# Inverse norms of queries and keys on 16 columns a projection, and one reciprocal of four columns a head

## The chip, the cores and the metric

The kernel runs on one core of a Trainium2 chip. The metric is the device time of one execution in microseconds (us). TensorE is called PE below, VectorE DVE, ScalarE ACT, GpSimd POOL; SP is the engine that issues most DMAs.

## What is computed

One sequence of 512 rows and 1024 features goes through two transformer blocks in fp32. The first mixes by a pooling branch and by 12 heads of dilated attention, the second by 4 differential heads, 6 forgetting heads and 6 chunk heads. Cut to what the change touches:

```python
# first block: softmax over the keys, per head
e = jnp.exp(s - m); den = jnp.sum(e, axis=-1, keepdims=True)
o = jnp.einsum('brnhqk,brnkhd->brnqhd', e / den, vb)
# second block: every head's query and key is normed over its 64 features
q1 = rms_norm_2(split_heads(q1, H_DIFF), g[0])   # and q2, k1, k2, qf, kf, qc, kc
a = probs(q1b, k1) - lam * probs(q2b, k2)        # differential heads
pr = jax.nn.softmax(s, axis=-1)                  # forgetting and chunk heads
```

## The kernel before

**Stages.** The program runs mixer 1 (0 to 200 us of the span), its output projection (to 280), a feed-forward part (to 600 and 640), mixer 2 (640 to 905), its output projection (to 960) and a last feed-forward part with the gate. Products of fp32 are built from three matmuls each (high by high, high by low, low by high parts of the operands; lines 189 to 191 and 366 to 368), so weights are split into `wh` and `wl` as they come in (L166 on ACT, L170 on DVE or POOL).

**Mixers.** A play list, `ORDER1` or `ORDER2`, says in which order steps are written. In mixer 2 the part that matters below is `S00 S01 F P2 T3 P4 T2 VA W00 T4 S10 W01`: S is the scores of a head, P a projection of 256 columns of queries and keys (`project`), T its transposes into head form (`to_heads`, L310), V the values, W the weighing (`weigh`: transposes of the probabilities L277, then L285 and L286). The build then fixes one order of instructions for each engine; it may move an instruction ahead of one that was written earlier where their tiles allow it.

**Scores.** `probs` handles one block of 128 queries (qb = 0 to 3, with 128, 256, 384 or 512 keys): two matmuls (L255, L256), a masked negative row maximum on DVE (L259) into column 0 of a small tile, the exponential on ACT with its row sum into column 1, and a reciprocal of that one column on DVE (L263). `scale_rows` (L267) multiplies the block by it on POOL. Differential heads (S00 to S11) make two blocks a qb; the second is multiplied by lambda and subtracted on DVE (L707, L708).

**Norm of queries and keys.** In `project` of mixer 2, two of the four row tiles share a PSUM bank, so `out_of` is called twice a projection with 512 columns. Each call copies (L659) and squares (L660) on ACT, reduces the squares to 8 columns on DVE (L662), makes the inverse root of these 8 columns (L665 to L673 on DVE, Ln and Exp on ACT) and multiplies the copy `z` by it on POOL (L675). The transposes of T read `z`.

**Small tiles.** `small(w)` (L118) hands out tiles of w columns from a ring for each w: 16 buffers of 4 columns, 16 of 8 columns. A tile of one ring does not wait for one of another.

Of the kernel before, what the change touches and what calls it, by code (L numbers as in the profile page):

```python
# [11 lines left out]
AF = mybir.ActivationFunctionType  # L12
ALU = mybir.AluOpType
AX = mybir.AxisListType

P = 128
# [46 lines left out]
class Builder:  # L63
# [52 lines left out]
        self.special.append(i.ins.name)  # L116

    def small(self, w=4, dt=F32):  # L118
        return self.mp.tile([P, w], dt, tag=f"m{w}", name=self.nm("m"), bufs=16 if w < 16 else 3 if w < 64 else 1)

    def psum(self, wide=False):
        if wide:
# [123 lines left out]
        self.rsqrt(r, ps[:, 0:8], 1.0 / D, self.small(8))  # L246
        return r

    def probs(self, op, tab, qb, wide=False):
        nc = self.nc  # L250
        q1, k1, q2, k2 = op
        n = (qb + 1) * P
        c = slice(qb * P, qb * P + P)
        ps = self.psum() if wide else self.psS()
        nc.tensor.matmul(ps[:, :n], lhsT=q1[:, c], rhs=k1[:, :n], start=True, stop=False)  # L255
        nc.tensor.matmul(ps[:, :n], lhsT=q2[:, c], rhs=k2[:, :n], start=False, stop=True)  # L256
        p = self.slot("p")
# [6 lines left out]
        return p, m  # L264

    def scale_rows(self, p, m, n):
        self.nc.gpsimd.tensor_scalar(p[:, :n], p[:, :n], m[:, 2:3], 1.0, ALU.mult, ALU.mult)  # L267

    def weigh(self, ps_list, v, o, odd, wide=False):
        nc = self.nc  # L270
# [19 lines left out]
        nc.vector.tensor_tensor(o[a, :], pv[a, :], t[a, :], ALU.add)  # L290

    def scores(self, op, tab, wide=False):
        out = []
        for qb in range(4):
            p, m = self.probs(op, tab, qb, wide)
            self.scale_rows(p, m, (qb + 1) * P)
            out.append(p)
        return out

    def play(self, order, **steps):  # L300
# [314 lines left out]
    def mix2(self, h, rc):  # L615
        nc = self.nc
# [5 lines left out]
        r2 = self.const("r2", [P, 4])  # L622
        r1 = self.const("r1", [P, 4])
# [8 lines left out]
        lam = self.const("lam", [P, 4])  # L632
# [14 lines left out]
        ops = {}  # L647
# [5 lines left out]

        def project(i):
            out = zs[i] = []

            def out_of(t1, ps):
                z, sq = self.slot("z"), self.slot("z")
                nc.scalar.activation(z, ps, AF.Copy)  # L659
                nc.scalar.activation(sq, ps, AF.Square)  # L660
                st = self.small(8)
                nc.vector.tensor_reduce(st, sq.rearrange("p (h d) -> p h d", d=64), AX.X, ALU.add)  # L662
                four = lambda v: v[:, t1 - 1:t1 + 1].unsqueeze(2).to_broadcast([P, 2, 4])
                two = lambda v: v.rearrange("p (t h) -> p t h", h=4)
                nc.vector.tensor_tensor(two(st), two(st), four(r2), ALU.mult)  # L665
# [6 lines left out]
                nc.vector.tensor_tensor(two(y), two(y), four(r1), ALU.mult)  # L672
                nc.vector.tensor_tensor(st, y, w, ALU.mult)  # L673
                zv = z.rearrange("p (h d) -> p h d", d=64)
                nc.gpsimd.tensor_tensor(zv, zv, st.unsqueeze(2).to_broadcast([P, 8, 64]), ALU.mult)  # L675
                out.append(z)
# [14 lines left out]
        def table(name, src):  # L691
            t = self.slot("m")
            self.load_late(t, src)
            tabs[name] = t
            return t

        def score(i, e, wide=False):
            n, e = int(i), int(e)
            if n < 2:
                tab = table("a", io["tab_alibi"][2 * n + e])  # L700
                out = []
                for qb in range(4):
# [4 lines left out]
                    nc.vector.tensor_scalar(m2[:, 3:4], m2[:, 2:3], lam[:, 2:3], None, ALU.mult)  # L707
                    nc.vector.scalar_tensor_tensor(p1[:, :w], p2[:, :w], m2[:, 3:4], p1[:, :w],  # L708
                                                   ALU.mult, ALU.add)
# [48 lines left out]
        def early(m):  # L758
# [264 lines left out]
```

## Time and profile before

| what | us |
|---|---|
| runs | 1356.41, 1363.6, 1360.2 |
| median | 1360.2 |
| profiled execution, own time | 1363.75 |
| its span | 1362.0 |
| PE busy | 1319.5 |
| DVE busy | 862.6 |
| ACT busy | 674.2 |
| POOL busy | 205.5 |

The profile is one execution. Busy time is the union of an engine's instructions; a busy PE can still run at the lower of its two clock levels. The clock that was granted stands as PEclk, 1.00 being 2.4 GHz. A wait is written with the instruction that waited, the engine and line that released it, and its length.

### The profile page before, as it was taken

What the parts mean: (1) busy time and instruction counts of PE and PEld (TensorE: products, weight loads), DVE (VectorE), ACT (ScalarE), POOL (GpSimd) and SP (SyncE); (2) the same over time, 40 slices, a digit from 0 to 9 for tenths busy, and PEclk for the clock granted to TensorE, in tenths of its full rate; (3) what the DMA queues carried; (4) which work ended last, traced back from release to release, by engine and by line L of the source; (5) the groups of instructions that cost most, each with busy time, mean ns of one, the idle gap of its engine ahead of it and who ended that gap; (6) DMA issues with size and microseconds to landing.
All of it is one profiled execution on the core that took longest, in us unless ns stands there. A gap on an engine that the chain in (4) does not pass through costs nothing.

```text
span 1362.0 us, 20144 instructions
## 1 busy us (share of the span) xinstructions
PE 1319.5 (97%) x7450; PEld 1146.2 (84%) x7450; DVE 862.6 (63%) x1739; ACT 674.2 (50%) x1311; POOL 205.5 (15%) x240
## 2 busy tenths in 40 slices
PE   9899999999999999997999999999999999999998
PEld 9899878888888888886989999778888888888887
DVE  6777876864444432239678978666877777733345
ACT  6566756543333333236476778654644444522242
POOL 1233222300000000016222434331000000000010
PEclk9999999999999999998999999899999999999999
DMA  5422333233232233326333544332423332323222
GB/s 196 121 70 60 105 117 97 74 101 100 94 93 93 93 95 101 98 78 224 94 107 99 140 118 130 90 116 86 139 94 96 101 98 93 101 93 93 95 91 78
DMA packets 48802, 141.70 MB, mean 104 GB/s; under 512 B 6240, under 2 KB 7136, under 8 KB 48704
## 3 DMA queue, kind: packets, MB, share of 16 engines
q1 hardware_dynamic: 48704, 140.42, 33.1%
q8 instruction: 58, 0.95, 0.3%
q14 instruction: 40, 0.33, 0.1%
HBM read 122.38 MB, written 6.29 MB: 94 GB/s over the span
## 4 chain that ended last, share of the span: by engine, by line
PE 83%; DVE 10%; DMA 2%; issue 2%; ACT 2%; POOL 0%; SPq 0%; DVEq 0%; ACTq 0%; POOLq 0%
PE p L190 21%; PE p L189 21%; PE p L191 20%; PE p L368 5%; PE p L367 5%; PE p L366 5%; PE p L277 2%; DVE wl L170 1%; DVE sp L259 1%; DVE sv L573 1%; DVE sh L183 1%; PE p L286 1%; PE p L285 1%; PE p L255 1%; PE p L256 1%
## 5 line engine op out<-in xcount | busy, mean ns | idle before, releaser
L166 ACT ACTIVATE wh<-wr 128x512 fp32r<-128x512 f32 x417 | 260.0, 630 | 401.2 <-PE p L190 348.4
L170 DVE TENSOR_TENSOR wl<-wr,wh 128x512 fp32r<-128x512 f32 x398 | 287.7, 728 | 224.0 <-ACT wh L166 217.8
L190 PE MATMUL p<-sh,wh 128*128 128x512 f32 (+1 forms) x858 | 324.2, 379 | 7.7 <-DVE sh L183 7.6
L191 PE MATMUL p<-sh,wl 128*128 128x512 f32 (+1 forms) x858 | 323.5, 378 | 0.0
L189 PE MATMUL p<-sh,wh 128*128 128x512 f32 (+1 forms) x858 | 318.9, 377 | 0.1
L366 PE MATMUL p<-wh,sh 128*128 128x256 f32 (+1 forms) x736 | 211.2, 289 | 4.3 <-ACT sz L460 2.2
L368 PE MATMUL p<-wh,sh 128*128 128x256 f32 (+1 forms) x736 | 210.2, 288 | 5.2 <-DVE sh L183 5.2
L367 PE MATMUL p<-wl,sh 128*128 128x256 f32 (+1 forms) x736 | 210.6, 288 | 0.2
L190 PEld LDWEIGHTS p<-sh,wh 128*128 128x128 f32 x858 | 163.6, 191 | 39.6 <-DVE sh L183 9.0
L191 PEld LDWEIGHTS p<-sh,wl 128*128 128x128 f32 x858 | 163.7, 191 | 31.4 <-issue 0.7
L189 PEld LDWEIGHTS p<-sh,wh 128*128 128x128 f32 x858 | 161.8, 191 | 32.1 <-PE p L256 0.6
L368 PEld LDWEIGHTS p<-wh,sh 128*128 128x128 f32 x736 | 141.4, 193 | 7.3 <-DVE sh L183 6.4
L366 PEld LDWEIGHTS p<-wh,sh 128*128 128x128 f32 x736 | 141.9, 193 | 6.3 <-ACT sz L460 2.5
L367 PEld LDWEIGHTS p<-wl,sh 128*128 128x128 f32 x736 | 141.8, 193 | 1.4 <-DVE wl L170 0.6
L267 POOL TENSOR_SCALAR sp<-sp,m 128x128 f32<-128x128 f32 (+1 forms) x112 | 70.3, 631 | 161.8 <-DVE m L263 122.9
L170 POOL TENSOR_TENSOR wl<-wr,wh 128x512 fp32r<-128x512 f32 (+1 forms) x19 | 25.3, 1329 | 450.6 <-ACT wh L166 441.7
L114 ACT ACTIVATE sp<-sp,m 128x128 f32<-128x128 f32 (+3 forms) x128 | 71.5, 559 | 40.8 <-DVE m L259 37.6
L191 PE MATMUL p<-so,wl 128*128 128x512 f32 (+1 forms) x246 | 88.4, 360 | 0.3 <-DVE wl L170 0.3
L190 PE MATMUL p<-so,wh 128*128 128x512 f32 (+1 forms) x246 | 88.4, 360 | 0.0
L189 PE MATMUL p<-so,wh 128*128 128x512 f32 (+1 forms) x246 | 87.7, 361 | 0.5 <-DVE m L259 0.5
L259 DVE CUSTOM_DVE_ANT_0 sp<-p,sm 128x128 f32<-128x128 f32 (+3 forms) x128 | 60.2, 483 | 19.5 <-PE p L256 9.6
L190 PE MATMUL p<-sk,wh 128*128 128x512 f32 (+1 forms) x184 | 67.1, 365 | 0.0
(207 smaller groups left out, 2100.8 us busy)
## 6 DMA issues: line engine op xcount, KB each, us to landing
wr<-in_w_gu SPq DMA_DIRECT2D x88, 512.0 KB
wr<-in_w_down SPq DMA_DIRECT2D x44, 512.0 KB
wr<-in_w_qk SPq DMA_DIRECT2D x31, 512.0 KB
sk<-sk SPq DMA_DIRECT2D x88, 128.0 KB
wr<-in_w_out SPq DMA_DIRECT2D x12, 512.0 KB
sv<-in_x SPq DMA_DIRECT2D x16, 256.0 KB
wr<-in_w_ple_gate SPq DMA_DIRECT2D x8, 512.0 KB
wr<-in_w_v SPq DMA_DIRECT2D x6, 512.0 KB
```

The source lines that it names most:

```text
L114: i = self.nc.scalar.activation(out, in_, func, **k)
L166: nc.scalar.activation(hi[:, :w], c, AF.Copy)
L170: eng.tensor_tensor(lo[:, :w], c, hi[:, :w].bitcast(F32), ALU.subtract)
L189: mm(out, lhsT=ahi, rhs=bhi, start=start, stop=False)
L190: mm(out, lhsT=ahi, rhs=blo, start=False, stop=False)
L191: mm(out, lhsT=alo, rhs=bhi, start=False, stop=stop)
L259: nc.vector.tensor_tensor_reduce(p[:, :n], ps[:, :n], tab[:, (3 - qb) * P:S], 1.0, 3e38, ALU.add, ALU.min, accum_out=m[:, 0:1])
L267: self.nc.gpsimd.tensor_scalar(p[:, :n], p[:, :n], m[:, 2:3], 1.0, ALU.mult, ALU.mult)
L277: ins = nc.tensor.transpose(pt[:, w:w + P], ps_list[qb][:, kb * P:kb * P + P], self.ident)
L366: mm(d, lhsT=h[k][0][:, a], rhs=hi[:, c], start=k == 0 and (o == 0 or not first), stop=False)
L367: mm(d, lhsT=h[k][0][:, a], rhs=lo[:, c], start=False, stop=False)
L368: mm(d, lhsT=h[k][1][:, a], rhs=hi[:, c], start=False, stop=k == 7 and (o > 0 or not first))
```

## The change

`probs` gets a small tile and a column from its caller. `scores` takes one tile of 16 columns a head, lets the four blocks write maxima to columns 0 to 3 and sums to columns 4 to 7, makes one reciprocal of four columns into columns 8 to 11, and then issues the four multiplications on POOL. Differential heads take one such tile for each qb and make one reciprocal of two columns. `project` of mixer 2 takes one tile of 16 columns, each of the two calls of `out_of` reduces into half of it, and at the second call the inverse root is made once on 16 columns, after which both halves of `z` are multiplied. The tiles of 16 columns, those of heads and those of projections, are one ring of 8 buffers.

```diff
-        ... bufs=16 if w < 16 else 3 if w < 64 else 1)
+        ... bufs=16 if w < 16 else 8 if w < 24 else 3 if w < 64 else 1)
...
-    def probs(self, op, tab, qb, wide=False):
+    def probs(self, op, tab, qb, m, j, wide=False):
...
-        m = self.small(4)
-            accum_out=m[:, 0:1])
-        self.act(p[:, :n], p[:, :n], AF.Exp, bias=m[:, 0:1], scale=-1.0, accum_out=m[:, 1:2])
-        nc.vector.reciprocal(m[:, 2:3], m[:, 1:2])
+            accum_out=m[:, j:j + 1])
+        self.act(p[:, :n], p[:, :n], AF.Exp, bias=m[:, j:j + 1], scale=-1.0, accum_out=m[:, 4 + j:5 + j])
...
     def scores(self, op, tab, wide=False):
+        m = self.small(16)
+        out = [self.probs(op, tab, qb, m, qb, wide) for qb in range(4)]
+        self.nc.vector.reciprocal(m[:, 8:12], m[:, 4:8])
         for qb in range(4):
-            p, m = self.probs(op, tab, qb, wide)
-            self.scale_rows(p, m, (qb + 1) * P)
+            self.scale_rows(out[qb], m, qb, (qb + 1) * P)
...
         def project(i):
+            st = self.small(16)
...
-                st = self.small(8)
-                nc.vector.tensor_reduce(st, sq.rearrange("p (h d) -> p h d", d=64), AX.X, ALU.add)
+                nc.vector.tensor_reduce(st[:, 4 * t1 - 4:4 * t1 + 4], sq.rearrange("p (h d) -> p h d", d=64),
+                                        AX.X, ALU.add)
+                out.append(z)
+                if t1 < 3:
+                    return
...
-                y, w = self.small(8), self.small(8)
+                y, w = self.small(16), self.small(16)
...
-                nc.gpsimd.tensor_tensor(zv, zv, st.unsqueeze(2).to_broadcast([P, 8, 64]), ALU.mult)
+                for j in range(2):
+                    zv = out[j].rearrange("p (h d) -> p h d", d=64)
+                    nc.gpsimd.tensor_tensor(zv, zv, st[:, 8 * j:8 * j + 8].unsqueeze(2).to_broadcast([P, 8, 64]),
+                                            ALU.mult)
...
-                    p1, m1 = self.probs(ops[2 * n][e], tab, qb, wide)
-                    p2, m2 = self.probs(ops[2 * n + 1][e], tab, qb, wide)
-                    self.scale_rows(p1, m1, w)
+                    m = self.small(16)
+                    p1 = self.probs(ops[2 * n][e], tab, qb, m, 0, wide)
+                    p2 = self.probs(ops[2 * n + 1][e], tab, qb, m, 1, wide)
+                    nc.vector.reciprocal(m[:, 8:10], m[:, 4:6])
+                    self.scale_rows(p1, m, 0, w)
```

The instructions fall from 128 reciprocals to 40 and from 120 small DVE instructions of the norms to 60; 40 Ln and Exp instructions on ACT become 20. PE, POOL and SP have the same instructions as before. Their order is the same outside the two mixers.

**PE, end of P4, T2 and VA.** In the rows `p` is a PSUM tile, `sz` a z tile, `sp` a block of probabilities, `m` a small tile, `sk` queries or keys; the numbers are of each build alone. Before, from the last matmul of P4 on:

```order
L368 MATMUL p_7298<-wh_7241,sh_5739 128x256
L310 MATMUL p_7364<-ident,sz_7167 128x128 x2
L310 MATMUL p_7364<-ident,sz_7101 128x128 x2
L310 MATMUL p_7365<-ident,sz_7167 128x128 x2
L310 MATMUL p_7365<-ident,sz_7101 128x128 x2
L277 MATMUL p_7524<-ident,sp_6866 128x128
L277 MATMUL p_7524<-ident,sp_6885 128x128
L277 MATMUL p_7535<-ident,sp_6866 128x128
L277 MATMUL p_7535<-ident,sp_6885 128x128 x2
L255 MATMUL p_6949<-sk_6787,sk_6786 128x384
L256 MATMUL p_6949<-sk_6788,sk_6786 128x384
L255 MATMUL p_6960<-sk_6815,sk_6814 128x512
```

After, up to the first matmul of VA (L275 is the transpose of probabilities, L308 that of `z`, L364 the first of the three matmuls of a projection or of values):

```order
L275 MATMUL p_7530<-ident,sp_6794 128x128
L275 MATMUL p_7530<-ident,sp_6811 128x128
L275 MATMUL p_7541<-ident,sp_6811 128x128
L275 MATMUL p_7530<-ident,sp_6828 128x128
L275 MATMUL p_7541<-ident,sp_6828 128x128
L275 MATMUL p_7530<-ident,sp_6845 128x128
L275 MATMUL p_7541<-ident,sp_6845 128x128 x2
L308 MATMUL p_7221<-ident,sz_7035 128x128 x2
L308 MATMUL p_7221<-ident,sz_6981 128x128 x2
L308 MATMUL p_7222<-ident,sz_7035 128x128 x2
L308 MATMUL p_7222<-ident,sz_6981 128x128 x2
L364 MATMUL p_7253<-wh_7256,sh_5652 128x256
```

T2's eight transposes of `z` stood right behind P4 and ahead of the last three scores of S01; now they stand behind S01's last scores and behind the transposes of S01's four probability blocks (sp_6794 to sp_6845). VA's matmuls, which stood between and behind S01's last scores, follow T2 in both.

**DVE, the second square sum of P2.** Before (ISA is the masked maximum of a score block, from its PSUM tile and the table sm into sp and a column of m):

```order
L259 ISA sp_6866,m_6867<-p_6863,sm_6823 128x384
L259 ISA m_6867 128x1
L259 ISA sp_6874,m_6875<-p_6871,sm_6823 128x384
L259 ISA m_6875 128x1
L662 TENSOR_REDUCE m_7171<-sz_7168 128x8
L323 SCALAR_TENSOR_TENSOR sk_7194<-p_7184,gq,sk_7194 64x512
L325 SCALAR_TENSOR_TENSOR sk_7196<-p_7185,gq,sk_7195 64x512
L665 TENSOR_TENSOR m_7171<-m_7171,r_6031 128x8
L263 RECIPROCAL m_6867<-m_6867 128x1
L263 RECIPROCAL m_6875<-m_6875 128x1
L707 TENSOR_SCALAR m_6875<-m_6875,lam 128x1
L259 ISA sp_6885,m_6886<-p_6882,sm_6823 128x512
```

After:

```order
L258 ISA sp_6834,m_6824<-p_6831,sm_6788 128x384
L258 ISA m_6824 128x1
L180 TENSOR_TENSOR st_7387<-p_7381,st_7386 128x512
L258 ISA sp_6845,m_6841<-p_6842,sm_6788 128x512
L258 ISA m_6841 128x1
L660 TENSOR_REDUCE m_6911<-sz_6982 128x8
L660 TENSOR_REDUCE m_6911<-sz_7036 128x8
L180 TENSOR_TENSOR st_7398<-p_7392,st_7397 128x512
L258 ISA sp_6851,m_6841<-p_6848,sm_6788 128x512
L258 ISA m_6841 128x1
```

The square sums of P2's halves (TENSOR_REDUCE; the second one before has m_7171) stood among S00's blocks, ahead of all of S01. Now both, in m_6911, stand behind the maximum of 512 keys in S01's last small tile, m_6841: in the order of the changed kernel the tiles of this one ring are first written in the order of the program, where S01 is ahead of P2.

**POOL, the multiplications of `z` for T2.** Before:

```order
L675 TENSOR_TENSOR sz_6750<-sz_6750,m_6754 128x512
L267 TENSOR_SCALAR sp_6828<-sp_6828,m_6829 128x128
L675 TENSOR_TENSOR sz_7101<-sz_7101,m_7105 128x512
L267 TENSOR_SCALAR sp_6847<-sp_6847,m_6848 128x256
L170 TENSOR_TENSOR wl_7422<-wr_7419,wh_7421 128x512
L267 TENSOR_SCALAR sp_6866<-sp_6866,m_6867 128x384
L267 TENSOR_SCALAR sp_6885<-sp_6885,m_6886 128x512
L675 TENSOR_TENSOR sz_7167<-sz_7167,m_7171 128x512
L267 TENSOR_SCALAR sp_6906<-sp_6906,m_6907 128x128
L267 TENSOR_SCALAR sp_6925<-sp_6925,m_6926 128x256
L675 TENSOR_TENSOR sz_7281<-sz_7281,m_7285 128x512
```

After:

```order
L265 TENSOR_SCALAR sp_6794<-sp_6794,m_6790 128x128
L265 TENSOR_SCALAR sp_6811<-sp_6811,m_6807 128x256
L170 TENSOR_TENSOR wl_7610<-wr_7607,wh_7609 128x512
L265 TENSOR_SCALAR sp_6828<-sp_6828,m_6824 128x384
L265 TENSOR_SCALAR sp_6845<-sp_6845,m_6841 128x512
L678 TENSOR_TENSOR sz_6981<-sz_6981,m_6911 128x512
L678 TENSOR_TENSOR sz_7035<-sz_7035,m_6911 128x512
L678 TENSOR_TENSOR sz_7150<-sz_7150,m_7080 128x512
L678 TENSOR_TENSOR sz_7204<-sz_7204,m_7080 128x512
```

The two halves for T2 were sz_7101 and sz_7167, the second of them behind S00's last block and ahead of S01's blocks; now they are sz_6981 and sz_7035, behind all four blocks of S01 (sp_6794 to sp_6845), with those of P4 right behind them.

## Rows read from the trace of the kernel before

**Rows 1.** The page, part 1: busy time of each engine over the span.

```profile
PE 1319.5 (97%) x7450; PEld 1146.2 (84%) x7450; DVE 862.6 (63%) x1739; ACT 674.2 (50%) x1311; POOL 205.5 (15%) x240
```

**Rows 2.** Windows, two stages: us; busy PE, PEld, DVE, ACT, POOL (xcount); PEclk; DMA share; GB/s.

```profile
25.00:200.00 175.00, 167.76 (x1203) 156.52 (x1202) 139.44 (x346) 107.78 (x244) 53.69 (x72) 0.98 0.31 92
...
640.00:905.00 265.00, 252.81 (x1866) 236.79 (x1866) 206.46 (x608) 182.99 (x437) 89.49 (x107) 0.97 0.37 109
```

**Rows 3.** The reciprocals, line L263: times of one, idle DVE before them.

```profile
L263 DVE RECIPROCAL m<-m x128: 133/157/167, 62.4 to 901.3; 128x1 f32<-128x1 f32 x128
...
  ACT sp L114: 10.2, 21
```

**Rows 4.** DVE groups by shape, 640 to 905: xcount, busy us, mean ns, idle before.

```profile
L170 DVE TENSOR_TENSOR wl<-wr,wh 128x512 fp32r<-128x512 f32 x44 | 35.1, 818 | 6.3 <-ACT wh L166 6.1
L180 DVE TENSOR_TENSOR st<-p,st 128x512 fp32r<-128x512 f32 x28 | 19.0, 684 | 1.5 <-ACT st L179 1.1
L259 DVE CUSTOM_DVE_ANT_0 sp<-p,sm 128x512 f32<-128x512 f32 x20 | 13.7, 683 | 0.7 <-PE p L256 0.4 <-PE p L368 0.3
L662 DVE TENSOR_REDUCE m<-sz 128x8 f32<-128x512 f32 x20 | 13.6, 678 | 2.8 <-ACT sz L660 2.7
...
L259 DVE CUSTOM_DVE_ANT_0 sp<-p,sm 128x384 f32<-128x384 f32 x20 | 10.8, 549 | 2.3 <-PE p L277 2.1
...
L669 DVE SCALAR_TENSOR_TENSOR m<-m,m 128x8 f32<-128x8 f32 x20 | 5.5, 276 | 2.2 <-ACT m L114 2.1
...
L708 DVE SCALAR_TENSOR_TENSOR sp<-sp,m,sp 128x512 f32<-128x512 f32 x4 | 3.8, 946 | 0.1
...
L670 DVE TENSOR_TENSOR m<-m,m 128x8 f32<-128x8 f32 x20 | 3.5, 176 | 0.3
...
L708 DVE SCALAR_TENSOR_TENSOR sp<-sp,m,sp 128x384 f32<-128x384 f32 x4 | 2.5, 614 | 0.1
```

**Rows 5.** POOL groups by shape, 640 to 905.

```profile
L675 POOL TENSOR_TENSOR sz<-sz,m 128x512 f32<-128x512 f32 x20 | 22.6, 1131 | 39.4 <-DVE m L673 37.3 <-DMA wr<-in_w_qk 1.6 <-DVE m L707 0.4
...
L267 POOL TENSOR_SCALAR sp<-sp,m 128x512 f32<-128x512 f32 x16 | 11.9, 743 | 15.9 <-DVE m L263 6.6 <-DVE m L669 3.6 <-DVE m L670 2.2
```

**Rows 6.** What PE waited for, 640 to 905: us, times, longest.

```profile
PE p L255 <- DVE m L259: 3.8, 5, 1.7
...
PE p L277 <- DVE sp L708: 1.0, 1, 1.0
...
PE p L277 <- DVE m L263: 0.7, 1, 0.7
```

**Rows 7.** Timeline, 717 to 727: start, us, engine, line, operation [idle before, releaser].

```profile
717.94 0.15 DVE L263 RECIPROCAL m<-m 128x1 f32<-128x1 f32 x1
...
718.01 0.14 DVE L669 SCALAR_TENSOR_TENSOR m<-m,m 128x8 f32<-128x8 f32 x1
...
718.56 1.03 PE L310 MATMUL p<-ident,sz 128*128 128x128 f32 x8
...
719.43 0.71 PE L277 MATMUL p<-ident,sp 128*128 128x128 f32 x5
719.58 1.04 POOL L675 TENSOR_TENSOR sz<-sz,m 128x512 f32<-128x512 f32 x1 [0.91 <-DVE m L673]
...
719.70 1.47 DVE L170 TENSOR_TENSOR wl<-wr,wh 128x512 fp32r<-128x512 f32 x1
...
721.57 0.68 DVE L170 TENSOR_TENSOR wl<-wr,wh 128x512 fp32r<-128x512 f32 x1
...
721.70 0.50 PE L255 MATMUL p<-sk,sk 128*128 128x512 f32 x1 [1.21 <-DVE m L259]
```

**Rows 8.** Windows around three places of mix2, columns as in Rows 2.

```profile
862.00:872.00 10.00, 6.87 (x36) 4.85 (x35) 7.52 (x30) 6.61 (x20) 5.82 (x9) 0.87 0.40 133
872.00:880.00 8.00, 8.00 (x37) 6.87 (x36) 6.07 (x16) 6.42 (x15) 1.87 (x3) 0.74 0.18 42
...
700.00:718.70 18.70, 18.70 (x154) 18.35 (x153) 16.89 (x62) 13.44 (x36) 6.30 (x8) 1.00 0.26 80
```

More of the change, by code (lines that the diff above doesn't have):

```diff
@@ L118, in small @@
     def small(self, w=4, dt=F32):
-        return self.mp.tile([P, w], dt, tag=f"m{w}", name=self.nm("m"), bufs=16 if w < 16 else 3 if w < 64 else 1)
+        return self.mp.tile([P, w], dt, tag=f"m{w}", name=self.nm("m"), bufs=16 if w < 16 else 8 if w < 24 else 3 if w < 64 else 1)
     def psum(self, wide=False):
@@ L257, in probs, with scale_rows @@
         p = self.slot("p")
-        m = self.small(4)
         nc.vector.tensor_tensor_reduce(
             p[:, :n], ps[:, :n], tab[:, (3 - qb) * P:S], 1.0, 3e38, ALU.add, ALU.min,
-            accum_out=m[:, 0:1])
-        self.act(p[:, :n], p[:, :n], AF.Exp, bias=m[:, 0:1], scale=-1.0, accum_out=m[:, 1:2])
-        nc.vector.reciprocal(m[:, 2:3], m[:, 1:2])
-        return p, m
-    def scale_rows(self, p, m, n):
-        self.nc.gpsimd.tensor_scalar(p[:, :n], p[:, :n], m[:, 2:3], 1.0, ALU.mult, ALU.mult)
+            accum_out=m[:, j:j + 1])
+        self.act(p[:, :n], p[:, :n], AF.Exp, bias=m[:, j:j + 1], scale=-1.0, accum_out=m[:, 4 + j:5 + j])
+        return p
+    def scale_rows(self, p, m, j, n):
+        self.nc.gpsimd.tensor_scalar(p[:, :n], p[:, :n], m[:, 8 + j:9 + j], 1.0, ALU.mult, ALU.mult)
     def weigh(self, ps_list, v, o, odd, wide=False):
@@ L292, in scores @@
     def scores(self, op, tab, wide=False):
-        out = []
+        m = self.small(16)
+        out = [self.probs(op, tab, qb, m, qb, wide) for qb in range(4)]
+        self.nc.vector.reciprocal(m[:, 8:12], m[:, 4:8])
         for qb in range(4):
-            p, m = self.probs(op, tab, qb, wide)
-            self.scale_rows(p, m, (qb + 1) * P)
-            out.append(p)
+            self.scale_rows(out[qb], m, qb, (qb + 1) * P)
         return out
@@ L660, in out_of @@
                 nc.scalar.activation(sq, ps, AF.Square)
-                st = self.small(8)
-                nc.vector.tensor_reduce(st, sq.rearrange("p (h d) -> p h d", d=64), AX.X, ALU.add)
-                four = lambda v: v[:, t1 - 1:t1 + 1].unsqueeze(2).to_broadcast([P, 2, 4])
-                two = lambda v: v.rearrange("p (t h) -> p t h", h=4)
-                nc.vector.tensor_tensor(two(st), two(st), four(r2), ALU.mult)
-                y, w = self.small(8), self.small(8)
+                nc.vector.tensor_reduce(st[:, 4 * t1 - 4:4 * t1 + 4], sq.rearrange("p (h d) -> p h d", d=64),
[3 more added lines that the diff above has]
+                    return
+                each = lambda v: v.unsqueeze(2).to_broadcast([P, 4, 4])
+                heads = lambda v: v.rearrange("p (t h) -> p t h", h=4)
+                nc.vector.tensor_tensor(heads(st), heads(st), each(r2), ALU.mult)
+                y, w = self.small(16), self.small(16)
                 self.act(y, st, AF.Ln, bias=self.eps, scale=1.0)
@@ L671, in out_of @@
                 nc.vector.tensor_scalar(w, w, -0.5, 1.5, ALU.mult, ALU.add)
-                nc.vector.tensor_tensor(two(y), two(y), four(r1), ALU.mult)
+                nc.vector.tensor_tensor(heads(y), heads(y), each(r1), ALU.mult)
                 nc.vector.tensor_tensor(st, y, w, ALU.mult)
-                zv = z.rearrange("p (h d) -> p h d", d=64)
-                nc.gpsimd.tensor_tensor(zv, zv, st.unsqueeze(2).to_broadcast([P, 8, 64]), ALU.mult)
-                out.append(z)
+                for j in range(2):
+                    zv = out[j].rearrange("p (h d) -> p h d", d=64)
+                    nc.gpsimd.tensor_tensor(zv, zv, st[:, 8 * j:8 * j + 8].unsqueeze(2).to_broadcast([P, 8, 64]),
+                                            ALU.mult)
             self.chunk("w_qk2", int(i), h, 256, out_of)
@@ L703, in score @@
                     w = (qb + 1) * P
-                    p1, m1 = self.probs(ops[2 * n][e], tab, qb, wide)
-                    p2, m2 = self.probs(ops[2 * n + 1][e], tab, qb, wide)
-                    self.scale_rows(p1, m1, w)
-                    nc.vector.tensor_scalar(m2[:, 3:4], m2[:, 2:3], lam[:, 2:3], None, ALU.mult)
-                    nc.vector.scalar_tensor_tensor(p1[:, :w], p2[:, :w], m2[:, 3:4], p1[:, :w],
+                    m = self.small(16)
[3 more added lines that the diff above has]
+                    self.scale_rows(p1, m, 0, w)
+                    nc.vector.tensor_scalar(m[:, 12:13], m[:, 9:10], lam[:, 2:3], None, ALU.mult)
+                    nc.vector.scalar_tensor_tensor(p1[:, :w], p2[:, :w], m[:, 12:13], p1[:, :w],
                                                    ALU.mult, ALU.add)
```

## The prediction

> **What bounds the kernel now.** I read the busy times first: PE is busy for 97% of the span, DVE for 63% [rows 1]. So an instruction that DVE no longer makes is worth nothing by itself; it counts only where PE stands still for DVE, or for POOL behind it. The windows by stage say where that can be. In mixer 1, PE is idle for 175.0 - 167.8 = 7.2 us of its stretch, in mixer 2 for 265.0 - 252.8 = 12.2 us [rows 2]. That is 19.4 us in all, and the change touches no other stage. In mixer 2 DVE is busy for 206.5 of 265 us (78%). The waits of PE there are short and scattered; the largest group is scores that wait for a masked maximum to free a PSUM bank, 3.8 us in five cases, and transposes waited for a reciprocal once, for 0.7 us [rows 6]. So the most that all edits together can give is under 19.4 us, and one new wait of PE of some 10 us takes back more than they can be expected to give. I therefore looked in the order of the changed kernel for places at which PE has little queued ahead of something that has moved later.
>
> **Fewer instructions on DVE.** A reciprocal takes 157 ns [rows 3]; 88 of them go, 52 in mixer 2 and 36 in mixer 1: 8.2 and 5.7 us. Of the small instructions of the norm, 60 go, each between 176 and 276 ns [rows 4]: 10.6 to 16.6 us, taken as 12.4. No row shows such an instruction on 16 columns. Between a reciprocal of one column at 157 ns and an instruction of eight at 176 the columns show little, so I take 16 at the price of 8; were they at twice the price, these 12.4 us would be nothing. DVE in mixer 2 thus falls from 206.5 to about 186 us, by 10%. DVE also stood idle 10.2 us in 21 cases in front of a reciprocal, waiting for the row sum of an exponential [rows 3], and most of these waits go too. What PE gets of that: of its 19.4 idle us, a part hangs on DMAs, on ACT and on the transitions of stages. With 10% less DVE work I take 2.5 us off; the ends are 0 (all of it lies in slack) and 5 (a quarter of all idle time). **-2.5 (0 to -5).**
>
> **Ln and Exp on ACT.** Twenty instructions of ACT go. ACT is busy 183 of 265 us in that stage [rows 2] and not what PE waits for there [rows 6]: nothing, and if its cover were gone it would only be a gain.
>
> **Later multiplications of the probabilities.** All four blocks of a head are now scaled behind its last exponential. The last scale comes behind three others, each at most 0.74 us [rows 5], so it ends up to 2.2 us later than it did. What hides it is the projection matmuls that the play order puts between S and W; PE met this edge once in mixer 2, for 0.7 us [rows 6]. In the order of the changed kernel the few heads whose transposes stood close to their last exponential now have more matmuls ahead of them, and four heads remain tight; I take the one 0.7 us again, and one whole late scale as the upper end. **+0.7 (0 to +2.2).**
>
> **The wait at T2.** This is the large term. P2's square sums now stand on DVE behind the last masked maxima of S01, since heads and projections share one ring, and on PE T2 stands behind S01's transposes, with VA's bulk of 96 matmuls behind T2. PE is in order, so VA, which needs nothing from T2, waits as well.
>
> What PE has left between the end of P4 and T2: 17 transposes, of which eight take 719.43 - 718.56 = 0.87 us [rows 7], so 0.109 each, 1.85 us; and three score blocks of 384, 512 and 512 columns, two matmuls each. The 154 matmuls of a full stretch came every 18.7/154 = 0.121 us [rows 8], mostly with 256 columns; by columns that is 1.3 us. Together 3.2 us.
>
> What DVE has to do from about that moment (it has just freed the bank of S01's first block of 384 columns): two weight splits at 0.68 (the undisturbed one, [rows 7]) 1.36; the combination of the 256-column block, taken as the 384 one, 0.61; a maximum of 384 columns 0.55; two of 512, 1.37; two probability splits (L180) 1.37 and one of half size, some 0.4; four square sums 2.71 (two of P2, and two of P4 that stand between); combinations of 384 and 512 columns 0.61 and 0.95 [rows 4]. That is 9.9 us. Twelve small ones come with it. They overlap: the reciprocal at 717.94 is followed by the next instruction 0.07 us later, although it is listed with 0.15 [rows 7]. At 0.1 each, 1.2 us. Then POOL multiplies both halves of z, 1.04 us each in the timeline [rows 7] and 1.13 in the mean [rows 5]: 2.1. Sum 13.2 us; less PE's own 3.2 it is a wait of 10.0 us, spread over the last transposes of S01 and T2. Before, PE lost 1.2 us at this place, the score at 721.70 [rows 7]. Net **+8.8**. The low end counts only what cannot start before S01's last score has been read: two square sums, both combinations, the small ones and POOL, 6.6 us, less the ten transposes that PE then still has, 1.1, less 1.2 from before: +4.3. The high end takes the means of rows 4 and 5 with DVE 1 us late: +11.5. I stay with the full sum because DVE had little room around this place before, busy for 16.89 of the 18.7 us ahead of it [rows 8].
>
> The rows show one price that could come on top. A weight split on DVE that began 0.12 us after a multiplication of z on POOL took 1.47 us, and 0.68 us two microseconds later without one [rows 7]. The Trainium skill, "SBUF — State Buffer", section "SBUF: two separate sides", says that a DVE instruction with two SBUF inputs and a GpSimd instruction that reads SBUF exclude each other for a whole instruction. The trace agrees, and it speaks against this change: the combinations and norm products of this chain have such inputs and stand among four scales and four multiplications now back to back; with one collision more the wait would be about 0.8 us longer, without one it stays as summed.
>
> **The clock behind that wait.** Around 862 to 872, where PE was busy only 6.87 of 10 us, the granted clock was 0.87, and 0.74 in the next 8 us, which is a stretch at the lower level (1.2 GHz) of the two; ahead of the 1.2 us stall at T2 it was 1.00 [rows 8]. After a stall of 10 us I expect the same fall: 8 x 0.26 = 2.1 us lost, with ends 0 and 3.4 (both windows). **+2.1 (0 to +3.4).** The Trainium skill, "TensorE: Matmul & The Clock Gate", section "Part 1: The HAM clock gate", has it that the slow state is the default and activity releases it; by that the term is not nothing, and the sum stays; without it the sum would be 2.1 less.
>
> **Sum.** 8.8 + 2.1 - 2.5 + 0.7 = +9.1 us. Against the profiled execution's own 1363.75 us that is 1372.9; it lies 3.5 us above the median of the runs. On the median of 1360.2 it is **1369.3 us**, 0.67% slower. A measurement of this kernel tells about 0.5% from no change, 6.8 us; so the bounds are 1353.4 and 1367.0.
>
> **Rivals.**
> A, the forecast: the wait at T2 is 7 to 12 us, and the clock falls behind it. 1365 to 1375.
> B, the wait is near its low end and the clock stays up: 4.3 - 2.5 + 0.7 = +2.5, 1362.7, or nothing at all with relief at its end: 1357 to 1366. For it: DVE has 1.5 us less ahead of this place, since P2's second square sum and its chain have moved behind it, and PE could do with fewer of the reads ahead of it. Against it: the reads of S01's last blocks come in DVE's order, between splits.
> C, faster: the wait at T2 isn't there, and the relief is at its end. It decides where DVE has passed the last combination of S01 by the time PE comes to its transposes, thus when PE is held on P4 for some 9 us by something else, such as weights that come late. Then relief of 5 and the 1.2 us from before give 1354, and a little more relief in mixer 1 than I count (all 7.2 us idle there in place of a part) 1349 to 1353.4. Against it: P4's matmuls ran without a gap before, 18.70 of 18.7 us busy [rows 8].
> D, more such places. Other projections share the ring with heads too (P5 with S11, P6 with S21 and S30, P9 with S60), and if one of them holds PE for 4 to 6 us as well, the time is 1374 to 1380. Against it: in the order PE has fill work there.
> E, the change does not shorten DVE: small instructions overlap so far that 148 fewer give half of what I count. That is in the end of the relief term: A without it, 1371.8.
>
> **How the numbers follow.** A with E 0.53, B 0.30, C 0.09, D 0.08. The range reaches from the low end of B to the early part of D, 1357 to 1377, leaving out C and half of D. Faster by over 0.5% is C, 0.09. Within 0.5%: B without its upper edge and the lower edge of A, 0.34. Slower: the rest, 0.57.
>
> **What would show it.** In the trace after: between 715 and 735 us, PE waits before the transposes of z (L308) or of S01's probabilities, released by POOL's multiplication of z (L678) or by DVE's L713 and L675, 7 to 12 us in all; a granted clock under 1 within the next ten microseconds; a DVE without a gap there; DVE busy in mixer 2 near 186 us; and PE's idle time outside that place lower by 2 to 3 us. The prediction is wrong if T2's eight transposes follow S01's transposes within 2 us, or if the small instructions on 16 columns take twice those on 8, or if the tail of mixer 2 (860 to 905), whose order is nearly as before, changes by more than 2 us.

## The result, and the profile after

The changed kernel takes 1369.74 us (median of 9 runs, 1365.2 to 1373.64); the kernel before takes 1361.13 us (9 runs). The ratio is 1.0055, 95% interval 1.0035 to 1.0075: slower by 0.55%. The two profiled executions lie closer together, 1366.93 against 1363.75 us, since single executions of either kernel scatter by some 8 us; the runs say by how much the kernels differ, the profiles where.

The busy times are the first line of the page. DVE lost 17 us against [rows 1] while PE's share is the same.

```profile
PE 1320.4 (97%) x7450; PEld 1143.8 (84%) x7450; DVE 845.3 (62%) x1591; ACT 669.9 (49%) x1291; POOL 203.0 (15%) x240
```

By stage (columns as in [rows 2]), mixer 1 gave nothing: PE's 167.81 of 175 us were 167.76. In mixer 2 PE is now busy for 248.60 of 265 us, with 1836 matmuls in place of 1866 in the same stretch. DVE is busy for 16 us less in that window, but the delay has pushed a part of the work out of it. Over the same 1866 matmuls (third line) DVE is busy for 194.15 us, 12.3 us less than before, and PE stands still for 16.4 us in place of 12.2.

```profile
25.00:200.00 175.00, 167.81 (x1193) 155.60 (x1194) 134.37 (x309) 107.57 (x244) 52.13 (x72) 0.98 0.31 92
...
640.00:905.00 265.00, 248.60 (x1836) 231.27 (x1836) 190.52 (x488) 173.89 (x405) 82.12 (x101) 0.96 0.37 108
...
639.70:910.46 270.76, 254.36 (x1866) 236.01 (x1866) 194.15 (x497) 179.25 (x417) 85.82 (x106) 0.96 0.37 107
```

The time is lost in one place. The windows around T2 show it (same columns). From 700 to 720 us PE has no gap. Then it is busy for 3.83 of 10.30 us, while DVE is busy for 10.13 of them, and for the 6.7 us behind that it is busy, but the granted clock is 0.54. Before, the same stretch had one stall of 1.2 us [rows 7].

```profile
700.00:720.00 20.00, 20.00 (x162) 19.28 (x160) 16.57 (x49) 15.95 (x39) 3.90 (x6) 1.00 0.37 107
720.00:730.30 10.30, 3.83 (x13) 1.76 (x12) 10.13 (x31) 5.03 (x15) 4.62 (x5) 0.63 0.25 62
730.30:737.00 6.70, 6.67 (x34) 6.68 (x35) 3.00 (x4) 2.73 (x4) 2.04 (x2) 0.54 0.40 105
737.00:745.00 8.00, 8.00 (x71) 8.00 (x70) 1.88 (x4) 2.39 (x5) 0.00 (x0) 1.00 0.02 5
...
718.26:730.33 12.07, 5.57 (x26) 3.04 (x24) 11.87 (x34) 6.65 (x19) 4.62 (x5) 0.69 0.34 94
```

The last line is the stretch from the end of P4 on PE to T2. What PE waited for from 715 to 740 us (us in total, times, longest), 6.5 us in all: combinations of S01's blocks on DVE, the split of transposed probabilities, and POOL's multiplication of z.

```profile
PE p L275 <- DVE sp L713: 2.4, 2, 1.6
PE p L275 <- DVE st L180: 2.2, 2, 2.0
PE p L308 <- POOL sz L678: 1.7, 1, 1.7
PE p L255 <- DVE m L258: 0.2, 1, 0.2
```

The timeline gives the chain (start, duration, engine, line, operation, and in brackets the idle time before and what ended it):

```profile
718.00 0.69 DVE L170 TENSOR_TENSOR wl<-wr,wh 128x512 fp32r<-128x512 f32 x1
...
718.26 0.60 PE L275 MATMUL p<-ident,sp 128*128 128x128 f32 x4
...
721.28 1.28 DVE L660 TENSOR_REDUCE m<-sz 128x8 f32<-128x512 f32 x2
...
723.30 0.66 PE L275 MATMUL p<-ident,sp 128*128 128x128 f32 x2 [1.99 <-DVE st L180]
...
725.45 1.27 DVE L660 TENSOR_REDUCE m<-sz 128x8 f32<-128x512 f32 x2
...
727.76 0.90 PE L275 MATMUL p<-ident,sp 128*128 128x128 f32 x3 [1.63 <-DVE sp L713]
...
727.90 0.17 DVE L675 TENSOR_TENSOR m<-m,m 128x16 f32<-128x16 f32 x1
...
728.22 2.05 POOL L678 TENSOR_TENSOR sz<-sz,m 128x512 f32<-128x512 f32 x2 [1.90 <-DVE m L672]
728.28 1.02 DVE L674 TENSOR_TENSOR m<-m,r 128x16 f32<-128x16 f32 x1
...
729.33 0.97 DVE L675 TENSOR_TENSOR m<-m,m 128x16 f32<-128x16 f32 x1
...
730.33 1.97 PE L308 MATMUL p<-ident,sz 128*128 128x128 f32 x8 [1.67 <-POOL sz L678]
```

DVE goes from its weight splits at 718.00 through the four square sums, two for T2 and two for T4, to the product that ends the inverse norm of T2's z at 727.90 (L675 of the changed kernel, under the listed 0.17 us). POOL multiplies both halves from 728.22 on in 2.05 us, and T2's transposes start at 730.33. They take 1.97 us where they took 1.03 [rows 7].

To see what this costs in all I compared the start of the matmul of the same rank, the n-th of the program, in both profiles (7450 of them in each). The changed kernel is 0.1 us ahead at 714.8 us of the span of before, 10.1 us behind at 729.9, 8.9 at 832, 8.6 at 860.5, 5.5 at 894 and 3.2 from 1041 to the end. So T2 costs 10 us in this pair of profiles, and 7 of them are given back later. Of these, 5.5 us (1.6, 2.4 and 1.5) come within three stretches in which before's granted clock was at the lower level; from 840 to 1041 us the changed kernel's was 1.00 (the first three lines are of the kernel before, the last of the changed kernel):

```profile
845.50:848.90 3.40, 3.40 (x18) 3.40 (x17) 3.37 (x10) 3.30 (x9) 1.68 (x3) 0.50 0.59 154
869.40:876.20 6.80, 6.09 (x25) 5.60 (x25) 4.73 (x14) 4.25 (x11) 3.47 (x5) 0.50 0.10 23
944.50:947.90 3.40, 3.40 (x18) 3.40 (x17) 3.40 (x7) 2.04 (x4) 0.00 (x0) 0.50 0.47 146
...
840.00:1041.00 201.00, 193.96 (x1097) 165.32 (x1096) 148.04 (x276) 119.11 (x234) 42.86 (x49) 1.00 0.34 108
```

Why the clock stays up in the changed kernel is not shown. PE stands still around the middle stretch there too, for 2.8 us from 868 to 888 as against 3.1 from 860 to 880 before. One pair of profiles can't tell how much of this comes back in every execution. For the middle stretch the profiles of the experiments below help, taken together with these two: in eight of them, the kernel before among them, PE waits neither at T2 nor for a filling, and seven of the eight have 6.8 us at the lower level that begin between 864 and 870 us. Neither of the two with the full wait at T2 has them. The other two stretches come and go among these profiles.

### The profile page after: what moved, and what is told of

The parts are those of the page before. It is cut to its first block, busy times and chain, and to the rows that moved or that the text cites. A ratio compares the mean times of both kernels' runs of the same rounds, so it can differ in the third digit from the quotient of the medians.

```text
span 1365.1 us, 19982 instructions
## 1 busy us (share of the span) xinstructions
PE 1320.4 (97%) x7450; PEld 1143.8 (84%) x7450; DVE 845.3 (62%) x1591; ACT 669.9 (49%) x1291; POOL 203.0 (15%) x240
## 4 chain that ended last, share of the span: by engine, by line
PE 83%; DVE 9%; ACT 2%; issue 2%; POOL 2%; DMA 2%; SPq 0%; DVEq 0%; ACTq 0%; POOLq 0%
PE p L190 20%; PE p L189 20%; PE p L191 20%; PE p L364 5%; PE p L366 5%; PE p L365 5%; PE p L275 2%; DVE wl L170 1%; DVE sv L571 1%; DVE sh L183 1%; DMA wr<-in_w_qk 1%; PE p L284 1%; PE p L255 1%; PE p L256 1%; PE p L283 1%
## 5 line engine op out<-in xcount | busy, mean ns | idle before, releaser
L170 DVE TENSOR_TENSOR wl<-wr,wh 128x512 fp32r<-128x512 f32 x398 | 284.3, 719 | 231.2 <-ACT wh L166 222.0
L364 PE MATMUL p<-wh,sh 128*128 128x256 f32 (+1 forms) x736 | 212.2, 290 | 4.7 <-ACT sz L458 2.3
L364 PEld LDWEIGHTS p<-wh,sh 128*128 128x128 f32 x736 | 142.5, 194 | 7.1 <-ACT sz L458 2.5
```

What stands on the lines that cost most here:

```text
L170: eng.tensor_tensor(lo[:, :w], c, hi[:, :w].bitcast(F32), ALU.subtract)
L364: mm(d, lhsT=h[k][0][:, a], rhs=hi[:, c], start=k == 0 and (o == 0 or not first), stop=False)
```

## The experiments

Each was measured in rounds against the kernel before on the same chip; a ratio stands with its 95% interval.

**A ring of its own for the norm.** The change with this alone:

```diff
-    def small(self, w=4, dt=F32):
-        return self.mp.tile([P, w], dt, tag=f"m{w}", ...
+    def small(self, w=4, dt=F32, ring="m"):
+        return self.mp.tile([P, w], dt, tag=f"{ring}{w}", ...
...
-            st = self.small(16)
+            st = self.small(16, ring="n")
-                y, w = self.small(16), self.small(16)
+                y, w = self.small(16, ring="n"), self.small(16, ring="n")
```

> The changed kernel with one difference: the tiles of 16 columns of the projections come from a ring of their own, those of the heads keep theirs. In its order T2's transposes of z stand again right behind P4, ahead of S01's last scores. Theory 'ring' (the slowdown is the wait at T2, which comes from sharing one ring): the waits of 8.1 us between 720 and 730 us and the low clock behind them are gone, and what is left is the relief of DVE, so 1356 to 1361 us against 1361.1 before, ratio 0.996 to 1.000, granted clock 1.00 from 700 to 740. Rival 'late scales' (all four scales of a head and both multiplications of z come later, ring or not): the time stays at 1367 to 1371.

Measured: 1360.82 us, ratio 0.9982 (0.9964 to 1.0000). Windows and T2's transposes of this kernel:

```profile
700.00:718.00 18.00, 18.00 (x149) 17.75 (x148) 16.57 (x53) 14.44 (x38) 6.29 (x8) 1.00 0.36 95
718.00:732.00 14.00, 14.00 (x118) 13.79 (x116) 13.42 (x32) 10.81 (x25) 3.90 (x5) 1.00 0.36 106
732.00:740.00 8.00, 6.95 (x56) 6.63 (x55) 7.52 (x21) 6.16 (x17) 2.85 (x3) 1.00 0.74 207
```

```profile
717.44 0.60 PE L308 MATMUL p<-ident,sz 128*128 128x128 f32 x4
...
718.23 0.60 PE L308 MATMUL p<-ident,sz 128*128 128x128 f32 x4
```

T2 runs at 717.44, some 13 us earlier than in the changed kernel, without a wait (in the changed kernel PE waited there for 6.5 us, not for the 8.1 of the expectation), PE has no gap from 700 to 732 us, and the clock stays at 1.00. Against the changed kernel's 1.0055 that is 0.73%, 9.9 us, by the ends of both intervals 5 to 15. The theory of the ring holds. It is the order of handing out that does it, not the number of buffers: with 24 buffers in the one ring the build gives the same order of PE and DVE, row for row, as with 8 (built only, not run).

**One ring in the kernel before.** Nothing merged, only the tiles shared:

```diff
-        m = self.small(4)
+        m = self.small(8, tag="mx")        # 32 buffers
...
-                st = self.small(8)
+                st = self.small(8, tag="mx")
```

> The kernel before, nothing merged, with one difference: the small tile of each score block and the tile into which a projection reduces its squares come from one ring of 32 tiles of 8 columns. In its order T2 stands behind S01's transposes, as in the changed kernel. Theory 'ring': the wait appears without any merging, 8 to 12 us with the low clock, and without relief: 1369 to 1374 us, ratio 1.006 to 1.009. Rival 'late scales': a ring alone does nothing, 1359 to 1363.

Measured: 1366.87 us, ratio 1.0033 (1.0019 to 1.0047); less than I expected. The wait is there in full, with the windows and waits of PE (715 to 740 us) much like those of the changed kernel:

```profile
718.00:732.00 14.00, 6.80 (x31) 4.46 (x30) 13.06 (x51) 8.09 (x23) 6.35 (x7) 0.65 0.30 95
732.00:740.00 8.00, 8.00 (x55) 8.00 (x55) 3.00 (x4) 2.46 (x4) 0.32 (x1) 0.75 0.28 66
```

```profile
PE p L277 <- DVE st L180: 2.3, 1, 2.3
PE p L310 <- POOL sz L675: 2.0, 1, 2.0
PE p L277 <- DVE sp L708: 1.5, 2, 1.1
PE p L277 <- DVE m L263: 1.3, 1, 1.3
```

By the ranks of matmuls this profile loses 10.4 us at T2 as well, 0.7 us ahead of before ahead of it and 9.8 behind after it. What I had left out is that a part comes back: 1.3 us around 775, and 1.5, 2.7 and 1.5 within before's three stretches at the lower clock; here the granted clock is 1.00 from 840 to 1041 us. A wait of DVE is a rival cause: in before's profile one masked maximum at 860.8 us waited 1.9 us for a table subtraction on POOL, and in the changed kernel DVE has no such wait in that part. The ranks don't bear it out. The changed kernel is 8.6 us behind at 860.5 and 9.1 at 868.9, and 2.4 of the 3.1 us given back from 860 to 905 come between 869.3 and 876.3, at before's lower clock.

It is not settled why the ring costs 2.6 to 6.4 us here and 5 to 15 in the changed kernel; the two intervals overlap from 5 to 6.

**The two parts alone.** First the reciprocals, with the norm as before:

```diff
         def project(i):            # all of the norm as in the kernel before
-            st = self.small(16)
...
+                st = self.small(8)
```

> The reciprocal part of the change alone: 16 columns a head and one reciprocal for its blocks, the norm of queries and keys as before on 8 columns from the ring of 8 columns. Theory 'ring': no wait at T2; 88 reciprocals less give 0 to 2 us, 1358 to 1361. Rival 'late scales': W waits for the later scales at several heads, 1363 to 1367.

Measured: 1365.37 us, ratio 1.0016 (1.0001 to 1.0031). No gain, and rather a loss; the profile has no wait at T2. Then the norm, with score blocks as before:

```diff
-        m = self.small(16)
-        out = [self.probs(op, tab, qb, m, qb, wide) for qb in range(4)]
+            p, m = self.probs(op, tab, qb, wide)      # small(4), one reciprocal a block
+            self.scale_rows(p, m, (qb + 1) * P)
```

> The norm part of the change alone: one inverse root on 16 columns a projection from a ring of 16 columns that nothing else uses, score blocks and reciprocals as before. Theory 'ring': no wait at T2, 60 small DVE instructions less give 0 to 3 us, 1358 to 1361. Rival 'late scales': the first half of z is multiplied later and T waits for it, 1363 to 1367.

Measured: 1356.28 us in 7 runs, ratio 0.9949 (0.9931 to 0.9968). This was better than expected, so it was measured again:

> The norm part alone once more, on the chip of the run with late scales. Theory: 0.993 to 0.997 of before again, 1354 to 1358 us. Rival: the first measurement of it rests on seven runs and was low by chance, 0.997 to 1.000.

1359.09 us in 12 runs, 0.9980 (0.9960 to 0.9999). The second interval hardly meets the first. The norm part alone is faster than before, by 0.5% in the first measurement and 0.2% in the second, of more runs; the second lies in the rival's range, so the first was probably low by chance.

**Which half of the reciprocal part costs.** The changed kernel with the norm's own ring, and in heads that are not differential one reciprocal and one scale for each block:

```diff
-        self.nc.vector.reciprocal(m[:, 8:12], m[:, 4:8])
-        for qb in range(4):
-            self.scale_rows(out[qb], m, qb, (qb + 1) * P)
+            self.nc.vector.reciprocal(m[:, 8:9], m[:, 4:5])   # in the loop over qb
+            self.scale_rows(p, m, 0, (qb + 1) * P)
```

> The changed kernel with the norm's own ring and, for heads that are not differential, one reciprocal and one scale for each block as soon as its exponential is done, as before; the pairs of the differential heads keep one reciprocal for two. The reciprocal part alone gave 1.0016 where the norm part alone gave 0.9949. Theory 'fours are late' (the four scales behind the last exponential cost what the reciprocals cost in all): near the norm part alone, 1355 to 1358. Rival 'pairs are late' (the first block of a pair is scaled after the second's exponential, and DVE's combination waits for it): 1359 to 1363.

Measured: 1359.08 us, 0.9980 (0.9967 to 0.9993). And the other way round, with single reciprocals in the differential heads:

```diff
-                    nc.vector.reciprocal(m[:, 8:10], m[:, 4:6])
+                    nc.vector.reciprocal(m[:, 8:9], m[:, 4:5])     # behind p1
+                    nc.vector.reciprocal(m[:, 9:10], m[:, 5:6])    # behind p2
```

> The changed kernel with the norm's own ring and two single reciprocals in place of one of two columns in the differential heads; the other heads keep one reciprocal of four columns and four scales behind it. Theory 'fours are late': 1359 to 1363. Rival 'pairs are late': 1355 to 1358.

Measured: 1359.97 us, 0.9990 (0.9973 to 1.0006). These two don't differ from each other, nor from the second measurement of the norm alone. By their times the first speaks for 'pairs are late' and the second for 'fours are late'. Both ranges stood on the 0.9949 that the second measurement did not bear out, so neither is shown. Last, the later place of the scales without any merged reciprocal:

```diff
-            p, m = self.probs(op, tab, qb, wide)
-            self.scale_rows(p, m, (qb + 1) * P)
+            out.append(self.probs(op, tab, qb, wide))
+        for qb in range(4):
+            self.scale_rows(*out[qb], (qb + 1) * P)
```

> The norm part alone (0.9949) with one thing more: in heads that are not differential the four scales are written behind the fourth block's reciprocal, each with its own reciprocal of one column. No reciprocal is merged. Theory 'late scales' (what the reciprocal part costs is the later place of the scales): 2 to 4 us above the norm part alone, 1358 to 1361. Rival 'other order' (it is the rest of the order that merging changes): the norm part's time, 1355 to 1358.

Measured: 1356.30 us, 0.9970 (0.9956 to 0.9984), beside 0.9980 for the norm alone on the same chip. In heads that are not differential, late scales cost nothing that can be seen (the two intervals leave room for some 2 us); as the cause of the slowdown that rival falls. Why the reciprocals alone end at 1.0016 stays open: the loss is 2 us, and no wait of PE in that profile belongs to a scaled block of mixer 2. In mixer 1 two do, 0.3 us each. The profiled execution took 1362.39 us, 3 us under the median, so it need not show the loss.

**Another order, same ring.** P2 written ahead of S01:

```diff
-    "... T1 T0 S00 S01 F P2 T3 P4 T2 VA W00 ..."
+    "... T1 T0 S00 P2 S01 F T3 P4 T2 VA W00 ..."
```

> The changed kernel, one shared ring, with P2 written ahead of S01 in the play order, so that its tile is handed out first. In its order P2's square sums stand ahead of S01's first maximum and T2 right behind P4. Theory 'ring': as with a ring of its own for the norm, 1357 to 1362 us against 1361.3, no wait over 2 us between 700 and 740. Rival 'late instructions' (the merged work itself makes T2 late): 1366 or more.

Measured: 1364.87 us, 1.0021 (1.0005 to 1.0037). T2's wait is gone, as in the theory, but the time is not that of a ring of its own: this order has smaller waits in other places (2.3 us at 844, 1.3 at 741). And VA ahead of T2:

```diff
-    "... P2 T3 P4 T2 VA W00 ..."
+    "... P2 T3 P4 VA T2 W00 ..."
```

> The changed kernel, one shared ring and P2's square sums as late as in it, with VA written ahead of T2, so that PE has VA's 96 matmuls (11.6 us) to do while DVE and POOL finish T2's input. Theory 'PE in order' (the wait costs only since nothing else stands in front of T2): 1357 to 1363 us. Rival: DVE has so much to do there that the wait moves on to W00 behind T2, 1366 or more.

Measured: 1367.04 us, 1.0033 (1.0016 to 1.0050). By the median the rival was right, but the runs lie in two groups: five took 1361.1 to 1363.2 us, about the theory's range, and seven 1366.4 to 1370.1. The profile is of one of the seven. T2 (L308) no longer waits, and then the second matmul of W00 waits for DVE's split of its probabilities, at the end of DVE's same queue:

```profile
733.51 1.04 PE L308 MATMUL p<-ident,sz 128*128 128x128 f32 x8
...
734.30 0.48 PE L283 MATMUL p<-st,sv 128*128 128x512 f32 x1
...
737.95 1.27 DVE L180 TENSOR_TENSOR st<-p,st 128x512 fp32r<-128x512 f32 x2
...
738.68 0.79 PE L284 MATMUL p<-st,sv 128*128 128x512 f32 x1 [3.90 <-DVE st L180]
```

The first lines are T2 and the first matmul of W00. L284 lost 3.90 us, for a split at 737.95 that stands in DVE's order behind the four splits of T2's heads. By ranks this profile loses 5.5 us between 730 and 750 us. VA's work hides the chain for T2 alone, not DVE's queue.

**Is the low clock part of the price?** Work without use, placed on PE in the wait:

```diff
+        for _ in range(fill):                  # T2 only: fill = 60, then 40
+            i = nc.tensor.matmul(qT[:, 0:P], lhsT=self.ones, rhs=self.ones, start=True, stop=True)
+            self.after(i.ins, self.last_score)
```

> The changed kernel with 60 matmuls of ones, 128 columns, whose product nothing uses, put on PE behind S01's last score and ahead of T2: some 6.5 us at 0.109 each, so about as long as the wait there. In its order T2 then stands ahead of the transposes of S01's probabilities. DVE's and POOL's work for T2 is the same, so T2 cannot start earlier than it did. Theory 'clock' (the wait costs its length and, behind it, 3.1 us at the lower clock level): the granted clock is 1.00 or nearly so from 720 to 740 where it was 0.63 and 0.54, and the time is 2 to 4 us under the changed kernel's 1369.7, so 1365 to 1368. Rival 'length only': 1369 to 1371.

Measured: 1374.95 us, 1.0099 (1.0082 to 1.0116), far from both. The filling was mis-sized: each of these matmuls shows as two records of 0.112 us, so they took twice as long as I reckoned, and T2 came at 737.32, 4 us after POOL had made its input (two multiplications of z from 731.15 on, 2.05 us).

```profile
723.92 13.56 PE L307 MATMUL p<-ones 128*128 128x128 f32 x120
737.32 1.04 PE L312 MATMUL p<-ident,sz 128*128 128x128 f32 x8
```

> As the run with 60 filling matmuls, with 40. There each filling matmul took two passes of 0.112 us, 13.4 us in all, and ended 4.1 us after POOL had made T2's input; 40 take 9.0 us and should end at about that moment. Theory 'clock': PE reaches T2 when its input is ready, as in the changed kernel, and runs on at the upper clock level, so the time is 1 to 4 us under the changed kernel's 1369.7 (the transposes of S01 behind T2 cost about 1.1 of the 3.1 gained): 1366 to 1369. Rival 'length only', the low clock behind the wait being given back later: 1369 to 1372.

Measured: 1368.46 us, 1.0040 (1.0022 to 1.0058), in two groups again, five runs at 1362.4 to 1364.8 us and seven at 1368.4 to 1371.3. Windows, the filling and POOL's multiplications of z (x2, ending at 733.43):

```profile
720.00:730.30 10.30, 10.09 (x84) 9.53 (x83) 9.75 (x30) 7.37 (x20) 3.05 (x4) 1.00 0.36 113
730.30:737.00 6.70, 6.70 (x62) 6.70 (x61) 5.36 (x13) 3.16 (x7) 4.09 (x4) 1.00 0.15 47
737.00:745.00 8.00, 8.00 (x71) 8.00 (x70) 2.48 (x5) 2.22 (x5) 0.00 (x0) 1.00 0.28 63
```

```profile
724.15 9.09 PE L307 MATMUL p<-ones 128*128 128x128 f32 x80
...
731.38 2.05 POOL L682 TENSOR_TENSOR sz<-sz,m 128x512 f32<-128x512 f32 x2 [1.90 <-DVE m L676]
```

The clock stays at 1.00 throughout, where the changed kernel had 0.63, 0.54 and 1.00. By ranks, the filling left out, the place costs 7.8 us here (3.3 behind before ahead of it, 11.1 after it) and 10.1 in the changed kernel. That is 2.3 us for the clock in the profiles; the runs say 0.15%, 2 us, but the intervals overlap and each group is wider than this. That the idle PE brought on the low clock at T2 is shown; that this costs 2 us in the end is likely, not settled.

## Why the prediction was right, and where its terms were off

**The forecast and its size.** Forecast 1369.3 us, measured 1369.74. The mechanism is the one named, case A: experiments with the ring alone move the wait in and out in both kernels. That the sum agrees to 0.4 us is luck. It was +9.1 us; the runs say +7.5 (4.8 to 10.2) by their ratio, and the median of before, 1360.2 us in three runs, became 1361.13 in nine. Its terms were off by more, in both directions.

**The wait at T2**, forecast 10.0 us and net 8.8. T2 began 12.1 us after PE's last matmul of P4 (718.26 is the next one's start, 730.33 T2's). Less the 3.2 us of PE's own work that is 8.9, net of the old stall 7.7. PE stood still for only 6.5 of the 12.1 us, though. It was busy for 5.57, not 3.2: its transposes came a few at a time, and the granted clock was 0.69 in this stretch. So a part of what the sum calls a wait was time of a PE at the lower clock. DVE's part was sized at 11.1 us and took 9.9 (718.00 to 727.90). Its large instructions are listed there with 9.5 us where I had 9.9, the two pairs of square sums with 1.28 and 1.27 instead of 1.36 each, and the small ones added some 0.4 us instead of 1.2. The collision that I had priced at 0.8 us and left out of the sum came at some 0.3: L667 took 0.47 us at 724.07, beside a scale on POOL from 723.94 to 724.53. POOL's 2.05 us were sized at 2.1. The parts listed for the low end add up to 6.2 us, not 6.6, so that end should have been +3.9.

**The signs.** The releasers, the fallen clock and a DVE without a gap (11.87 of 12.07 us) came as written. Others did not. The waits add up to 6.5 us, not 7 to 12. T2 followed the end of S01's transposes (727.76 and 0.90 us) by 1.67 us, and under 2 was to be a sign that I was wrong: the wait was spread over S01's transposes as well, and that sign was badly chosen. DVE's busy time for the work of mixer 2 is 194 us, not 186. PE's idle time there outside T2 fell from 11.0 to 9.9 us, by 1.1 and not by 2 to 3.

**Clock**, forecast +2.1. In the window behind the wait, 6.7 us at 0.54, some 3.1 us are lost. The Trainium skill, "TensorE: Matmul & The Clock Gate", section "Part 1: The HAM clock gate", says that the throttled state is the default and that activity releases it; the filled run agrees, with 1.00 in the same windows. What the term left out is the rest of the span: in the kernel before the clock is low later instead, and both profiled executions have the same mean granted clock, 0.985.

**The two together**: 10.9 forecast, 10.1 by the ranks, 5 to 15 by the runs with the ring undone. The step that failed is that PE gets none of it back: I wrote that a change of over 2 us in the part from 860 to 905 would speak against the prediction, and between the profiles that part became 3.1 us shorter. I had followed the loss only to where it arises, and not asked what becomes of the stalls and the low clock that the kernel before has behind it.

**Relief and late scales**, forecast -2.5 and +0.7, together -1.8: the changed kernel with its own ring is 2.5 us faster than before (0 to 4.9). The sum lies in that wide interval; the split between them was not right. Late scales are +0 by the run made for them, give or take 2 us. The relief comes from the norm; the reciprocals, 88 of the 148 instructions, give nothing that the runs show. DVE's work in mixer 2 fell by 12 us where 20 were forecast.

**Price of 16 columns**, taken as that of 8. DVE's lines in mixer 2 after (count, total, mean ns):

```profile
L675 DVE TENSOR_TENSOR m<-m,m 128x16 f32<-128x16 f32 x10 | 3.6, 355 | 0.2
...
L671 DVE SCALAR_TENSOR_TENSOR m<-m,m 128x16 f32<-128x16 f32 x10 | 3.1, 310 | 1.3 <-ACT m L114 1.2
...
L674 DVE TENSOR_TENSOR m<-m,r 128x16 f32<-128x16 f32 x10 | 2.5, 253 | 0.0
L667 DVE TENSOR_TENSOR m<-m,r 128x16 f32<-128x16 f32 x10 | 2.5, 248 | 0.1
...
L293 DVE RECIPROCAL m<-m 128x4 f32<-128x4 f32 x11 | 1.9, 176 | 3.3 <-ACT sp L114 3.3
...
L673 DVE TENSOR_SCALAR m<-m 128x16 f32<-128x16 f32 x10 | 1.7, 173 | 0.2
...
L672 DVE TENSOR_TENSOR m<-m,m 128x16 f32<-128x16 f32 x10 | 1.7, 171 | 0.2
```

L672 and L673 take 171 and 173 ns where the ones on 8 columns took 176 to 276 [rows 4], and the reciprocal of four columns 176 instead of 157 [rows 3]. So it holds for an undisturbed instruction. L667, L671, L674 and L675 have higher means, from a few long ones (below). All six together take 252 ns each where those on 8 columns took 207, and 9.7 us are saved by their rows in place of 12.4.

**The rivals.** B (a short wait) and C (none) fell with the windows. D (more such places) fell too: in mixer 2, beyond T2, no wait of PE over 1 us arose that before did not have. E, that 148 instructions less give half of what I counted, was half right: DVE's busy time fell by 17.3 us over the whole span, 12 in mixer 2 and 5 in mixer 1, which is two thirds of the 26.3 counted. In mixer 1 PE has nothing of it.

**A version that beats both.** The norm part with its own ring, everything else as before: 0.9949 and, with more runs, 0.9980 of before. It keeps the part from which the relief comes and has no shared ring.

## What to carry to other kernels

Merging small tiles can tie together steps that had nothing to do with each other: look at which tiles now come from one ring, and at the order in which the build lets them be written. Then ask at the consumer whether an engine that runs in order has anything else queued ahead of it; at its place the wait costs its length and the clock behind it, and what is left of it at the end of the program has to be measured. Fewer instructions on an engine that isn't the bound are worth what its waiters wait for it, here 2.5 us (0 to 4.9) for 148 instructions.

## What the runs showed of the hardware that I had not expected

A product on 16 columns took 1.02 us at 728.28 and the next 0.97 at 729.33, as against 0.17 a moment earlier; POOL was multiplying z from 728.22 to 730.27 (the timeline above). In the first filled run the same two took 1.02 and 0.96 beside the same POOL instructions. So a small instruction can take six times as long beside POOL. The Trainium skill, "SBUF — State Buffer", section "SBUF: two separate sides", says that DVE instructions with two SBUF inputs and GpSimd ones that read SBUF exclude each other for a whole instruction, and the trace agrees: both pieces lasted until about the end of a multiplication of 1.02 us.

A matmul of plain fp32 operands (`ones` by `ones`) showed as two records of 0.112 us, 80 for 40 instructions, while each transpose with the identity is one record.

The scatter of a kernel's runs goes with the clock: the changed kernel's run of 1365.2 us had a mean granted clock of 0.987, the one of 1373.64 us 0.981. A loss of 0.006 of 1370 us is an estimated 8.2 us, nearly all of the 8.4 between them. Where the clock falls differs between executions that do the same up to there. Near 689 us PE stands still for 1.8 us before, for 2.0 in the changed kernel and for 2.2 in the run with 40 filling matmuls. From 690 to 697 us the granted clock was 1.00, 1.00 and 0.51, and the last of the three is the 3.3 us by which that run was behind ahead of T2.
